# Taps, gates and modulation steps put in other places of a two-layer model with an RWKV block

## The chip, the cores and the metric

The kernel runs on one core of a Trainium2 chip. The metric is the device time of one execution in microseconds, taken as the median of several runs.

## The reference, cut to what matters

The input is one sequence of 256 positions with 1024 channels in float32. Two layers, each a mixer and a convolutional feed-forward block, are followed by a second block with adaptive modulation, an RWKV recurrence and a depthwise convolution.

```python
for i in range(2):                       # first block
    h = rmsnorm(x, norm_mix[i])
    x = x + (gla_mixer(h, ...) if i == 0 else attn_mixer(h, ...))
    x = x + conv_ffn(rmsnorm(x, norm_ffn[i]), ...)
def conv_ffn(h, w_up, w_conv, b_conv, w_down):
    u = conv3(h @ w_up) + b_conv         # depthwise, width 3
    val, gate = split(u)
    return (silu(gate) * val) @ w_down   # 2816 wide
# second block
mod = silu(c) @ ada_w + ada_b            # 1024 -> 3 x 1024
shift, scale, gate = split(mod)
h = rmsnorm(x, norm_g) * (1 + scale) + shift
c_val, c_gate, c_og, ts, r_og, g_conv, g_rwkv = split(h @ w_in)
u = causal_depthwise_conv(c_val * sigmoid(c_gate), conv_k) + conv_b  # 31 taps
y_conv = (silu(layernorm(u)) * silu(c_og)) @ w_conv_out
o = rwkv7_scan(token_shift(ts), ...)     # per head: state update, read-out
o = layernorm_per_head(o) + bonus
y_rwkv = (o * silu(r_og)) @ w_rwkv_out
m = sigmoid(g_conv) * y_conv + sigmoid(g_rwkv) * y_rwkv
x = x + gate * (m @ w_out)
out = rmsnorm(x, final_g)
```

## The kernel before, in words

Activations are kept with channels on the 128 partitions and the 256 positions along the free axis, in 8 chunks of 128 channels. Every large product is made in float32 accuracy from two reduced-precision parts, hi and lo, of both factors. `mm3` (L113 to L115) gives three products of 256 columns per chunk, `mm2` (L120, L123) one of 512 and one of 256 columns.

**Weights.** `Weights.load` (L77 to L80) brings each weight block into one of a ring of raw buffers by a DMA on SP's queue, strictly in program order (`issue_after`). ACT copies it to `hi` (L78), and DVE subtracts to get `lo` (L80). The DMA for a raw buffer waits until `lo` of the block that had the buffer last has been made.

**Order.** The kernel is written in one order. A scheduler arranges the instructions of each engine ahead of time. On the chip each engine runs its own list strictly in that order, so an instruction that waits holds up all that stand behind it.

**Stages.** The GLA mixer comes first: its rank products `gr` (L356) are the first that need weights, after warm-up products `warm` (L1331). Then `ffn0`, the attention layer and `ffn1`. A feed-forward block makes 22 pairs of `up` tiles with the width-3 convolution on ACT (L257) and DVE (L258, L259), a gated product `sg` (L263) and its split into `gg` (ACT L130, DVE L131), and then 8 `dn` tiles of 22 chunks each. `root_next` (L154) loads ACT's table of the square root ahead of the next norm.

**Modulation.** `ada` computes `silu(c) @ ada_w` in 24 steps of 1024 columns by 128 rows: a DMA of 512 KB into the same ring (`adaw`, L609) and one DVE instruction (L611 for the first of eight, L613 for the others). The table `AD` says after which loops of the stages a step is taken.

**The second block.** `inv` (from L845) inverts the triangular matrices of the recurrence on DVE, then makes the off-diagonal blocks by the cross products `zp` (L882) and `xp` (L892), with ACT copies between (L885, L874, L895). `chain` runs four chunks one after the other: `u`, the state `S` (`sp`, L924, then DVE L650), the output `op`, and after each second chunk the group norm `norm`, whose last step makes `yhi` (ACT L985) and `ylo` (DVE L990) for the products with `rwkv_out`. `fill` puts independent projections (`pj`) between these steps. The convolution has 8 channel chunks of 31 taps, each one DVE instruction (L1079, L1081). Chunks 5 to 7 (`CJ`) are bound behind the inverse. `cln` is its layer norm (`cmean` L1086, `nps_cv`, `rps_cv`) with the SiLU (L1095) and the gate `scog`, split into `yc`. `rout`, `cout` and `wout` are the last three projections. The gates are parked in DRAM and read back when wanted (`gri`, `gci`, `scogi`: DMA on SP, then a sigmoid or SiLU on ACT, L1010). `final` is the last norm with four output DMAs.

## Time and profile before

| what | value |
|---|---|
| median of 3 runs (lowest to highest) | 1013.92 us (1012.06 to 1015.05) |
| the profiled execution's own time | 1013.54 us |
| its span in the trace | 1011.7 us |
| mean granted TensorE clock | 0.983 of full |
| TensorE (PE) busy | 974.7 us, 96% |
| VectorE (DVE) busy | 832.3 us, 82% |
| ScalarE (ACT) busy | 611.0 us, 60% |
| bytes moved | 175.01 MB, mean 173 GB/s |

PE is busy for all but some 37 us of the span. A busy PE is not always at full speed: the granted clock is 0.5 or thereabouts in some short stretches, and there the same products take longer. So both the idle time and these stretches are to be read, and both are small against the span.

### The profile page before, as it was taken

Reading aid. Unit: us, or ns where it says so; the run is one execution under the profiler, and the core shown is the slowest. Engines: PE = TensorE matmul, PEld = TensorE weight load, DVE = VectorE, ACT = ScalarE, POOL = GpSimd, SP = SyncE. Lnnn points to the kernel's source line nnn. Section 1 sums busy time; section 2 is a strip of 40 time slices with the busy share of each in tenths; the row PEclk is TensorE's granted clock in tenths of the full one; section 3 lists DMA queues with packets and bytes.
Section 4 is the critical chain, followed back from the end, with each engine's and each line's share of the span. In section 5 each row is a group of like instructions: output and inputs, shape, how many; then the busy total and the mean of one; then the engine's idle time right before and its main releaser. Section 6 shows DMA issues by size and latency. Waiting matters only on the chain.

```text
span 1011.7 us, 19352 instructions
## 1 busy us (share of the span) xinstructions
PE 974.7 (96%) x7636; PEld 905.8 (90%) x7636; DVE 832.3 (82%) x1529; ACT 611.0 (60%) x1052; POOL 5.1 (0%) x15
## 2 busy tenths in 40 slices
PE   8999999999999999999999999999999999999796
PEld 7988899999888877999999889999988998898795
DVE  5956589888867886998888667999899898889795
ACT  6635666666544567676666456545676646745663
POOL 0000000000000000000000000000000000000000
PEclk8999999999999999999999999999999998999898
DMA  7738155556776861546656675455432362436451
GB/s 267 256 122 277 50 182 187 188 178 190 223 219 217 276 215 42 180 157 218 180 183 174 188 249 199 149 187 180 157 106 84 93 222 92 154 115 199 162 161 42
DMA packets 54442, 175.01 MB, mean 173 GB/s; under 512 B 6320, under 2 KB 12976, under 8 KB 53968
## 3 DMA queue, kind: packets, MB, share of 16 engines
q1 hardware_dynamic: 50464, 169.51, 52.7%
q10 hardware_dynamic: 3888, 4.27, 1.2%
q8 instruction: 60, 0.98, 0.4%
q14 instruction: 30, 0.25, 0.1%
HBM read 168.51 MB, written 5.24 MB: 172 GB/s over the span
## 4 chain that ended last, share of the span: by engine, by line
PE 79%; DVE 10%; DMA 4%; ACT 4%; issue 2%; ACTq 0%; DVEq 0%; SPq 0%
PE pj L113 8%; PE pj L115 8%; PE pj L114 8%; PE dn L120 8%; PE up L114 7%; PE up L115 7%; PE up L113 7%; PE pj L120 4%; PE dn L123 4%; DVE lo L80 3%; PE pj L123 2%; DMA adaw<-ada_w 2%; PE pt L113 2%; PE pt L114 2%; PE pt L115 2%
## 5 line engine op out<-in xcount | busy, mean ns | idle before, releaser
L78 ACT CAST hi<-raw 128x1024 fp32r<-128x1024 f32 (+2 forms) x286 | 295.0, 1034 | 243.2 <-PE pj L114 82.6
L80 DVE TENSOR_TENSOR lo<-raw,hi 128x1024 fp32r<-128x1024 f32 (+2 forms) x286 | 344.0, 1205 | 78.3 <-ACT hi L78 70.7
L114 PE MATMUL up<-h_f,hi 128*128 128x256 f32 x640 | 181.4, 284 | 0.5 <-DVE h_f L131 0.5
L113 PE MATMUL up<-h_f,hi 128*128 128x256 f32 x640 | 180.8, 283 | 0.3 <-ACT h_f L130 0.3
L115 PE MATMUL up<-h_f,lo 128*128 128x256 f32 x640 | 180.8, 283 | 0.0
L115 PE MATMUL pj<-h_s,lo 128*128 128x256 f32 x544 | 156.1, 287 | 1.7 <-DVE lo L80 1.7
L113 PE MATMUL pj<-h_s,hi 128*128 128x256 f32 x544 | 157.4, 290 | 0.0
L114 PE MATMUL pj<-h_s,hi 128*128 128x256 f32 x544 | 156.2, 287 | 0.0
L120 PE MATMUL dn<-gg,hi 128*128 128x512 f32 x352 | 124.9, 402 | 0.0
L114 PEld LDWEIGHTS up<-h_f,hi 128*128 128x128 f32 x640 | 122.8, 192 | 1.1 <-DVE h_f L131 1.1
L113 PEld LDWEIGHTS up<-h_f,hi 128*128 128x128 f32 x640 | 122.6, 192 | 0.5 <-ACT h_f L130 0.5
L115 PEld LDWEIGHTS up<-h_f,lo 128*128 128x128 f32 x640 | 122.8, 192 | 0.0
L115 PEld LDWEIGHTS pj<-h_s,lo 128*128 128x128 f32 x544 | 104.8, 193 | 2.6 <-DVE lo L80 1.9
L113 PEld LDWEIGHTS pj<-h_s,hi 128*128 128x128 f32 x544 | 104.9, 193 | 1.5
L114 PEld LDWEIGHTS pj<-h_s,hi 128*128 128x128 f32 x544 | 104.9, 193 | 1.1 <-issue 0.3
L1081 DVE SCALAR_TENSOR_TENSOR y<-u,long,y 128x233 f32<-128x233 f32 (+27 forms) x240 | 99.7, 469 | 0.7
L123 PE MATMUL dn<-gg,lo 128*128 128x256 f32 x352 | 97.1, 283 | 2.5 <-ACT gg L130 2.5
L120 PEld LDWEIGHTS dn<-gg,hi 128*128 128x128 f32 x352 | 66.2, 190 | 15.1
L123 PEld LDWEIGHTS dn<-gg,lo 128*128 128x128 f32 x352 | 67.0, 191 | 4.3 <-ACT gg L130 3.1
L257 ACT ACTIVATE y<-up,const 128x256 f32<-128x256 f32 x80 | 44.2, 556 | 1.9 <-DVE y L259 1.8
L259 DVE SCALAR_TENSOR_TENSOR y<-up,const,y 128x255 f32<-128x255 f32 x80 | 38.1, 479 | 1.2
L258 DVE SCALAR_TENSOR_TENSOR y<-up,const,y 128x255 f32<-128x255 f32 x80 | 37.9, 477 | 0.7 <-ACT y L257 0.7
(464 smaller groups left out, 1831.3 us busy)
## 6 DMA issues: line engine op xcount, KB each, us to landing
raw<-w_up SPq DMA_DIRECT2D x88, 512.0 KB, 4.1
raw<-w_down SPq DMA_DIRECT2D x32, 448.0 KB, 3.5
adaw<-ada_w SPq DMA_DIRECT2D x24, 512.0 KB, 4.5
raw<-w_down SPq DMA_DIRECT2D x16, 512.0 KB, 4.0
raw<-w_cvg SPq DMA_DIRECT2D x16, 512.0 KB, 4.1
raw<-gla_v SPq DMA_DIRECT2D x8, 512.0 KB, 5.1
raw<-gla_g SPq DMA_DIRECT2D x8, 512.0 KB, 3.7
raw<-gla_out SPq DMA_DIRECT2D x8, 512.0 KB, 4.8
```

The source lines that it names most:

```text
L78: nc.scalar.copy(hi[:, :w], raw[:, :w])
L80: nc.vector.tensor_tensor(out=lo[:, :w], in0=raw[:, :w], in1=hi[:, :w].bitcast(F32), op=ALU.subtract)
L113: nc.tensor.matmul(ps, lh, rh, start=start, stop=False)
L114: nc.tensor.matmul(ps, lh, rl, start=False, stop=False)
L115: nc.tensor.matmul(ps, ll, rh, start=False, stop=stop)
L120: wide = lambda: nc.tensor.matmul(ps, lhs[0], both, start=first, stop=last)
L123: nc.tensor.matmul(ps[:, 0], lhs[1], both[:, 0], start=False, stop=False)
L257: nc.scalar.activation(yb, ps[:, b, :], AF.Identity, scale=cw[:, 1, c:c + 1], bias=cw[:, 3, c:c + 1])
L258: nc.vector.scalar_tensor_tensor(out=yb[:, 1:], in0=ps[:, b, :T - 1], scalar=cw[:, 0, c:c + 1], in1=yb[:, 1:], op0=ALU.mult, op1=ALU.add)
L259: nc.vector.scalar_tensor_tensor(out=yb[:, :T - 1], in0=ps[:, b, 1:], scalar=cw[:, 2, c:c + 1], in1=yb[:, :T - 1], op0=ALU.mult, op1=ALU.add)
L1081: nc.vector.scalar_tensor_tensor(out=y[:, i:], in0=u[:, :T - i], scalar=w[:, j, 30 - i:31 - i], in1=y[:, i:], op0=ALU.mult, op1=ALU.add)
```

## The change

Seven edits are made at once.

- `gr`: two small products that nobody reads are put after each of the first seven chunks, six after the last (`g.idle`). `rstd_cols` runs its products in another order.
- `AD`: `ffn0` takes six modulation steps rather than eight, `ffn1` two rather than none; attention still takes eight, but each is two further on in the count.
- Convolution taps: chunks 5 to 7 come first, handed out in portions of 12, 6, 6 and eight times 8 inside `inv` and `chain` (`taps`); chunks 0 to 4 follow. The products `cmean` of chunks that are done are then free to stand in the chain.
- `zp`: the loop over halves is outside the loop over banks, and each bank and half has its own copy at once.
- `wout`: the square root's table is loaded after the last gate, and the last tile is made by `mm3` with one accumulator rather than `mm2` with two.
- `final`: five output DMAs, the last of one chunk, rather than four, the last of two.
- A switch that was off (`CT`) goes away.

```diff
@@ -157,9 +157,9 @@
 def rstd_cols(g, acc, name, eps=EPS):
 
     ps = g.ps.tile([P, 512], F32, name=f"nps_{name}")
-    for t in range(2):
-        for a in acc:
-            g.nc.tensor.matmul(ps[:, 2 * t:2 * t + 2], a[:, t * P:(t + 1) * P], g.ones[:, :2], start=a is acc[0], stop=a is acc[-1])
+    for a in acc:
+        for t in range(2):
+            g.nc.tensor.matmul(ps[:, 2 * t:2 * t + 2], a[:, t * P:(t + 1) * P], g.ones[:, :2], start=a is acc[0] and t == 0, stop=a is acc[-1], skip_group_check=True)
     return rsqrt(g, ps[:, :4], 1.0 / D, eps, name)
 
 
@@ -356,6 +356,7 @@
     ps = g.ps.tile([P, 512], F32, name="gr")
     for k in range(KD):
         mm3(nc, ps[:64, :T], (wh[:, k, :], wl[:, k, :]), (h[0][:, k, :], h[1][:, k, :]), k == 0, k == KD - 1)
+        g.idle(2 if k < KD - 1 else 6)
     for d in range(2):
         rows = slice(32 * d, 32 * d + 16)
         nc.vector.tensor_tensor(out=rT[rows, :], in0=ps[rows, :T], in1=rstd[rows, :], op=ALU.mult)
@@ -588,7 +589,7 @@
     out_project(g, I["attn_out"], o2)
 
 
-AD = dict(zip(("g", "f0", "a", "f1"), "11111111,11111111,11111111,00000000".split(",")))
+AD = dict(zip(("g", "f0", "a", "f1"), "11111111,00111111,11111111,00110000".split(",")))
 
 
 def step(g, where, i):
@@ -637,7 +638,6 @@
 CV = 16
 CJ = 5
 LAG = 2
-CT = 0
 PRE = dict(zip(("g", "f0", "a", "f1"), "00000000,00000000,00000000,00000000".split(",")))
 TB = 2
 ORDER = "low cvg pr pk pv prep inv gains chain cog gr gc conv cln rout cout wout"
@@ -874,15 +874,14 @@
             nc.scalar.copy(TTm[p0:p0 + 32, :, 32 * dg:32 * dg + 32], TD[p0:p0 + 32])
         zt = X2[:, 0]
         fill(1)
-        for b in range(2):
-            zp = psum.tile([P, 16, 32], F32, name=f"zp{b}")
-            for i in range(16):
-                for hf in range(2):
-                    o = 64 * hf + 32
-                    nc.tensor.matmul(zp[o:o + 32, i, :], Lb[64:96, hf, b, i, 32:], X2[64:96, hf, 16 * b + i, :], start=True, stop=True)
-            for hf in range(2):
-                o = 64 * hf + 32
-                nc.scalar.copy(zt[o:o + 32, 16 * b:16 * b + 16, :], zp[o:o + 32])
+        taps(12)
+        zp = [psum.tile([P, 16, 32], F32, name=f"zp{b}") for b in range(2)]
+        for hf in range(2):
+            o = 64 * hf + 32
+            for b in range(2):
+                for i in range(16):
+                    nc.tensor.matmul(zp[b][o:o + 32, i, :], Lb[64:96, hf, b, i, 32:], X2[64:96, hf, 16 * b + i, :], start=True, stop=True)
+                nc.scalar.copy(zt[o:o + 32, 16 * b:16 * b + 16, :], zp[b][o:o + 32])
             fill(1)
         for b in range(2):
             xp = psum.tile([P, 16, 32], F32, name=f"xp{b}")
@@ -894,6 +893,7 @@
                 o = 64 * hf
                 nc.scalar.copy(TTm[o:o + 32, 16 * b:16 * b + 16, 32:], xp[o:o + 32])
             fill(1)
+            taps(6)
 
 
     def chain():
@@ -917,6 +917,7 @@
                 for i in range(2):
                     nc.scalar.copy(VU[64:128, c, 8 * b + i:8 * b + 8:2, :], up[64 * i:64 * i + 64, i::2, :])
             fill(FC[2 * c])
+            taps(8)
             if c < 3:
                 sp = psum.tile([P, KD, 64], F32, name=f"sp{c}")
                 for hd in range(16):
@@ -940,6 +941,7 @@
             v.done = nc.scalar.copy(v.OT[:, :, cs], op)
             S = Sn
             fill(FC[2 * c + 1])
+            taps(8)
             if c % 2:
                 norm(c2)
 
@@ -1007,7 +1009,7 @@
         def get(j):
             t = sb.tile([P, T], F32, tag=name + "i", name=f"{name}i{j}")
             g.w.after(t, d[:, j, :])
-            nc.scalar.activation(t, t, f)
+            v.gate = nc.scalar.activation(t, t, f)
             return t
 
         setattr(v, name, get)
@@ -1060,25 +1062,38 @@
         for _ in range(CV):
             next(gates["cvg"])
 
-    def conv():
-        with ExitStack() as es:
-            conv_taps(es)
-
-    def conv_taps(es):
+    def chunks(js, es=None):
+
+        w = cst["conv_k"]
+        for j in js:
+            y, u = v.y[j], v.u[j]
+            behind = lambda: g.tc.issue_after(v.inv.ins) if j >= CJ else ExitStack()
+            with behind():
+                nc.vector.tensor_scalar(out=y, in0=u, scalar1=w[:, j, 30:31], scalar2=cst["conv_b"][:, j:j + 1], op0=ALU.mult, op1=ALU.add)
+            yield
+            for i in range(1, 31):
+                with behind():
+                    nc.vector.scalar_tensor_tensor(out=y[:, i:], in0=u[:, :T - i], scalar=w[:, j, 30 - i:31 - i], in1=y[:, i:], op0=ALU.mult, op1=ALU.add)
+                yield
+
+    def late():
         rest("cvg")
         v.ya = full("y")
         v.y = [v.ya[:, j, :] for j in range(KD)]
-        w = cst["conv_k"]
-        for j in range(KD):
-            y, u = v.y[j], v.u[j]
-            if j == CJ:
-                es.enter_context(g.tc.issue_after(v.inv.ins))
-            if CT:
-                nc.scalar.activation(y, u, AF.Identity, scale=w[:, j, 30:31], bias=cst["conv_b"][:, j:j + 1])
-            else:
-                nc.vector.tensor_scalar(out=y, in0=u, scalar1=w[:, j, 30:31], scalar2=cst["conv_b"][:, j:j + 1], op0=ALU.mult, op1=ALU.add)
-            for i in range(1, 31):
-                nc.vector.scalar_tensor_tensor(out=y[:, i:], in0=u[:, :T - i], scalar=w[:, j, 30 - i:31 - i], in1=y[:, i:], op0=ALU.mult, op1=ALU.add)
+        yield from chunks(range(CJ, KD))
+
+    late = late()
+
+    def taps(n):
+
+        for _ in range(n):
+            next(late, None)
+
+    def conv():
+        for _ in late:
+            pass
+        for _ in chunks(range(CJ)):
+            pass
 
     def cln():
         mps = bank("cmean")
@@ -1123,14 +1138,16 @@
         gated(I["conv_out"], v.yc, v.gc)
 
     def wout():
+        root_next(g, v.gate)
         g.x = full("x2")
         g.w.after(g.x, g.xs)
 
-        def ev(j, ps):
-            for b in range(2):
+        def ev(j, ps, n=2):
+            for b in range(n):
                 nc.vector.scalar_tensor_tensor(out=g.x[:, j, :], in0=ps[:, b], scalar=g.mod[:, 16 + j:17 + j], in1=g.x[:, j, :], op0=ALU.mult, op1=ALU.add)
 
-        project_both(g, I["w_out"], v.mh, ev)
+        project_both(g, I["w_out"][:KD - 1], v.mh, ev)
+        project(g, I["w_out"][KD - 1:], (v.mh[:, 0], v.mh[:, 1]), lambda j, ps: ev(KD - 1, ps.unsqueeze(1), 1))
 
     steps = dict(low=low, pk=pk, pr=pr, pv=pv, prep=prep, inv=inv, chain=chain, gains=gains, cvg=cvg, conv=conv, cln=cln,
                  rout=rout, cout=cout, wout=wout)
@@ -1147,7 +1164,7 @@
     r = rstd_cols(g, sumsq(g, "final"), "final")
     scale(KD - 1)
     rstd = spread(g, r, "final")
-    for a, n in ((0, 1), (1, 2), (3, 3), (6, 2)):
+    for a, n in ((0, 1), (1, 2), (3, 2), (5, 2), (7, 1)):
         o = g.sb.tile([P, n, T], F32, name=f"out{a}")
         nc.vector.tensor_tensor(out=o, in0=xg[:, a:a + n, :], in1=rstd.unsqueeze(1).to_broadcast([P, n, T]), op=ALU.mult)
         nc.sync.dma_start(g.O["outT"][:, a:a + n, :], o)
@@ -1327,8 +1344,12 @@
         nc.scalar.preload_act_table(AF.Silu)
         nc.vector.memset(g.ones, 1.0)
         warm = g.ps.tile([P, P], F32, name="warm")
-        for _ in range(WARM):
-            nc.tensor.matmul(warm, g.ones, g.ones, start=True, stop=True)
+        def idle(n):
+            for _ in range(n):
+                nc.tensor.matmul(warm, g.ones, g.ones, start=True, stop=True)
+
+        g.idle = idle
+        idle(WARM)
         nc.scalar.activation(g.silu_c, cst, AF.Silu)
         g.cst = {}
         g.cst["norm_mix0"], g.cst["ident"] = first[:, :KD], first[:, KD:]
```

DVE where `ffn1` passes from its last `up` tiles to its first `dn` tiles (`lo`: weight blocks; `gg`: the split of the gated product; `x<-dn`: the finished tile), before:

```order
L131 TENSOR_TENSOR gg_4506<-sg_20_6060,gg_4506 128x256
L259 SCALAR_TENSOR_TENSOR y_1_21_6126<-up_21_6065,const_3541,y_1_21_6126 128x255
L80 TENSOR_TENSOR lo_6230<-raw_6228,hi_6229 128x896
L258 SCALAR_TENSOR_TENSOR y_1_21_6130<-up_21_6065,const_3541,y_1_21_6130 128x255
L259 SCALAR_TENSOR_TENSOR y_1_21_6130<-up_21_6065,const_3541,y_1_21_6130 128x255
L80 TENSOR_TENSOR lo_6250<-raw_6248,hi_6249 128x896
L263 TENSOR_TENSOR sg_21_6134<-sg_21_6134,y_1_21_6126 128x256
L131 TENSOR_TENSOR gg_4506<-sg_21_6134,gg_4506 128x256
L276 TENSOR_TENSOR x<-dn_0_6140,x 128x256 x2
```

and now:

```order
L80 TENSOR_TENSOR lo_6234<-raw_6232,hi_6233 128x896
L131 TENSOR_TENSOR gg_4510<-sg_20_6064,gg_4510 128x256
L258 SCALAR_TENSOR_TENSOR y_1_21_6134<-up_21_6069,const_3545,y_1_21_6134 128x255
L259 SCALAR_TENSOR_TENSOR y_1_21_6134<-up_21_6069,const_3545,y_1_21_6134 128x255
L80 TENSOR_TENSOR lo_6254<-raw_6252,hi_6253 128x896
L263 TENSOR_TENSOR sg_21_6138<-sg_21_6138,y_1_21_6130 128x256
L614 SCALAR_TENSOR_TENSOR ada_3924<-adaw_7_6343,long,ada_3924 128x1024
L131 TENSOR_TENSOR gg_4510<-sg_21_6138,gg_4510 128x256
L276 TENSOR_TENSOR x<-dn_0_6144,x 128x256 x2
```

The last `ada` step of `ffn1` stands between `sg_21` and `gg_21`. In `ffn0` the order was `ada` (step 3), `sg_21`, `gg_21`, and is now `sg_21`, `gg_21`, `ada` (step 1).

DVE ahead of the products with `rwkv_out` (`OT`: the recurrence's output, `y<-u`: a tap), before:

```order
L1081 SCALAR_TENSOR_TENSOR y<-u,long,y 128x240
L1081 SCALAR_TENSOR_TENSOR y<-u,long,y 128x239
L650 TENSOR_TENSOR OT<-OT,gnb_10316 128x4x128
L1081 SCALAR_TENSOR_TENSOR y<-u,long,y 128x238
L650 TENSOR_TENSOR OT<-OT,srog 128x4x128
L650 TENSOR_TENSOR OT<-OT,gnb_10329 128x4x128
L984 TENSOR_TENSOR OT<-OT,vf 128x4x128
L650 TENSOR_TENSOR OT<-OT,srog 128x4x128
L1081 SCALAR_TENSOR_TENSOR y<-u,long,y 128x237
L984 TENSOR_TENSOR OT<-OT,vf 128x4x128
L990 TENSOR_TENSOR ylo<-OT,yhi 128x1024 x2
```

and now:

```order
L1076 SCALAR_TENSOR_TENSOR y<-u,long,y 128x229
L80 TENSOR_TENSOR lo_10912<-raw_10910,hi_10911 128x1024
L650 TENSOR_TENSOR OT<-OT,gnb_10425 128x4x128
L1076 SCALAR_TENSOR_TENSOR y<-u,long,y 128x228
L650 TENSOR_TENSOR OT<-OT,srog 128x4x128
L650 TENSOR_TENSOR OT<-OT,gnb_10438 128x4x128
L986 TENSOR_TENSOR OT<-OT,vf 128x4x128
L650 TENSOR_TENSOR OT<-OT,srog 128x4x128
L1076 SCALAR_TENSOR_TENSOR y<-u,long,y 128x227
L986 TENSOR_TENSOR OT<-OT,vf 128x4x128
L992 TENSOR_TENSOR ylo<-OT,yhi 128x1024
L1076 SCALAR_TENSOR_TENSOR y<-u,long,y 128x226
L992 TENSOR_TENSOR ylo<-OT,yhi 128x1024
```

The subtraction for a weight block stands ahead of the first `OT<-OT,gnb`, a tap stands between the two `ylo`, and on ACT a table load and a gate stand between the two `yhi`.

ACT from the SiLU of the convolution branch on (L1010, now L1012: a gate; L1095, now L1110: the SiLU), before:

```order
L143 ACTIVATE r_cv<-m_cv 128x4
L78 CAST hi_11182<-raw_11181 128x1024
L1095 ACT_TABLE_LOAD
L1095 ACTIVATE y<-y,long 128x256 x3
L130 CAST yc_10718<-y 128x256 x2
L1095 ACTIVATE y<-y,long 128x256 x2
L130 CAST yc_10718<-y 128x256
L1095 ACTIVATE y<-y,long 128x256 x2
L1010 ACTIVATE scogi_10746<-scogi_10746 128x256
L1010 ACTIVATE scogi_10754<-scogi_10754 128x256
L1095 ACTIVATE y<-y,long 128x256
L130 CAST yc_10718<-y 128x256 x2
```

and now, the end of the same stretch:

```order
L1110 ACTIVATE y<-y,long 128x256
L130 CAST yc_10738<-y 128x256 x2
L1012 ACTIVATE scogi_10782<-scogi_10782 128x256
L1110 ACTIVATE y<-y,long 128x256
L1012 ACT_TABLE_LOAD
L1012 ACTIVATE gri_11081<-gri_11081 128x256
L130 CAST yc_10738<-y 128x256
L1012 ACT_TABLE_LOAD
L1012 ACTIVATE scogi_10790<-scogi_10790 128x256
L1012 ACTIVATE scogi_10798<-scogi_10798 128x256
L78 CAST hi_11088<-raw_11087 128x1024
L130 CAST yc_10738<-y 128x256 x2
```

Before, one table load (`ACT_TABLE_LOAD`) stands between `r_cv` and the last `yc`; now there are four (two stand in the rows left out), and the cast of `hi_11088`, the first weight block of `conv_out`, stands behind all four. Before, the cast of that block stood ahead of `r_cv`.

## Rows read from the trace of the kernel before

**Rows 1.** The page, part 1: busy us (share of the span) and instructions.
```profile
PE 974.7 (96%) x7636; PEld 905.8 (90%) x7636; DVE 832.3 (82%) x1529; ACT 611.0 (60%) x1052; POOL 5.1 (0%) x15
```

**Rows 2.** By stretch: PE, PEld, DVE, ACT, POOL busy (instructions), granted clock, DMA.
```profile
820.00:830.00 10.00, 10.00 (x86) 10.00 (x85) 9.73 (x17) 5.90 (x8) 0.00 (x0) 1.00 0.94 307
15.60:20.70 5.10, 5.10 (x25) 5.10 (x26) 2.69 (x5) 2.36 (x3) 0.00 (x0) 0.50 0.94 343
280.00:283.50 3.50, 3.50 (x13) 2.94 (x13) 2.89 (x4) 1.22 (x2) 0.00 (x0) 0.52 0.43 129
949.10:956.00 6.90, 5.06 (x21) 4.71 (x21) 3.62 (x11) 4.34 (x11) 0.00 (x0) 0.51 0.76 273
```

**Rows 3.** What PE waited for, whole span: total us, times, longest.
```profile
PE pj L113 <- ACT yc L130: 4.5, 2, 3.5
...
PE dn L123 <- ACT gg L130: 2.5, 1, 2.5
...
PE kTp L531 <- DVE akr L483: 1.5, 1, 1.5
...
PE pj L114 <- DVE ylo L990: 1.3, 1, 1.3
...
PE rps_cv L170 <- DVE r_cv L147: 1.2, 1, 1.2
```

**Rows 4.** Timeline of PE at the start: start, us, line, out<-in, count [idle before].
```profile
4.62 1.92 PE L1331 MATMUL warm<-long 128*128 128x128 f32 x8
...
11.70 0.38 PE L113 MATMUL pj<-ph_g,hi 128*128 128x256 f32 x1 [1.27 <-ACT hi L78]
...
13.04 0.39 PE L115 MATMUL pj<-ph_g,lo 128*128 128x256 f32 x1 [0.84 <-DVE lo L80]
```

**Rows 5.** Timeline of DVE ahead of the down products of ffn0.
```profile
277.27 1.28 DVE L613 SCALAR_TENSOR_TENSOR ada<-adaw,long,ada 128x1024 f32<-128x1024 f32 x1 [2.71 <-DMA adaw<-ada_w]
```

**Rows 6.** Timeline of SP there.
```profile
272.29 0.33 SPq L609 DMA_DIRECT2D adaw<-ada_w  x1
```

**Rows 7.** Timeline of DVE ahead of the down products of ffn1.
```profile
551.84 1.09 DVE L80 TENSOR_TENSOR lo<-raw,hi 128x896 fp32r<-128x896 f32 x1
...
556.19 0.42 DVE L131 TENSOR_TENSOR gg<-sg,gg 128x256 fp32r<-128x256 f32 x1 [0.61 <-ACT gg L130]
```

**Rows 8.** Timeline of ACT around the cross products zp.
```profile
844.81 4.22 ACT L874 COPY TT<-LT 32x1024 f32<-32x1024 f32 x4
```

**Rows 9.** Timeline of DVE after the inverse, to the first chain state.
```profile
848.90 8.73 DVE L1081 SCALAR_TENSOR_TENSOR y<-u,long,y 128x255 f32<-128x255 f32 x22
861.10 0.69 DVE L650 TENSOR_TENSOR S<-sp,long 128x512 f32<-128x512 f32 x1 [3.46 <-PE sp L924]
```

**Rows 10.** Timeline of PE ahead of the first rwkv_out tile.
```profile
915.59 3.18 PE L1086 MATMUL cmean<-y,long 128*128 128x256 f32 x14
```

**Rows 11.** Timeline of DVE there.
```profile
911.91 1.22 DVE L80 TENSOR_TENSOR lo<-raw,hi 128x1024 fp32r<-128x1024 f32 x1
...
919.48 2.36 DVE L990 TENSOR_TENSOR ylo<-OT,yhi 128x1024 fp32r<-128x1024 f32 x2
```

**Rows 12.** Timeline of ACT between the convolution norm and the first conv_out tile.
```profile
946.05 1.28 ACT L1095 ACT_TABLE_LOAD   x1
947.66 1.58 ACT L1095 ACTIVATE y<-y,long 128x256 f32<-128x256 f32 x3 [0.34 <-DVE y L650]
949.99 0.74 ACT L130 CAST yc<-y 128x256 fp32r<-128x256 f32 x2 [0.74 <-DVE y L650]
...
954.88 0.72 ACT L1010 ACTIVATE scogi<-scogi 128x256 f32<-128x256 f32 x2 [1.82 <-DMA scogi<-scogd]
```

**Rows 13.** Timeline of ACT at the final norm.
```profile
1001.85 1.28 ACT L143 ACT_TABLE_LOAD   x1
```

**Rows 14.** Timeline of DVE there.
```profile
999.98 1.00 DVE L1131 SCALAR_TENSOR_TENSOR x<-pj,long,x 128x256 f32<-128x256 f32 x2 [0.51 <-PE pj L120]
...
1005.53 2.48 DVE L1152 TENSOR_TENSOR out<-xg,rps_final 128x256 f32<-128x256 f32 x4 [1.38 <-PE rps_final L170]
```

## The prediction

> **What bounds the kernel now.** I read the page first: PE is busy for 974.7 of 1011.7 us, 96% [rows 1], so nearly all of the time is products that the change leaves alone (it adds 20 small ones). What can move is PE's idle time and the stretches at the lower clock. The stretches came second. At full clock 86 products took 10.00 us, 0.116 each; at granted clock 0.50, 25 took 5.10 us, 0.204 each [rows 2]. So a busy microsecond at the lower level (1.2 rather than 2.4 GHz) loses 1 - 0.116/0.204 = 0.43 us. Third came PE's waits, which name the seams: the SiLU branch (`yc`, 4.5 in two waits), `gg` (2.5), `akr` (1.5), `ylo` (1.3), `r_cv` (1.2) [rows 3]. The low-clock stretches behind `gg` and behind `r_cv` and `yc` are in [rows 2], and single waits of 1.3 to 1.5 have none there. Last I read the lists of DVE, ACT and SP at these seams. Because PE's work stays, each term below is idle time or low clock that goes or comes. A plus is a gain.
>
> **The start.** 20 idle products are added. Eight took 1.92 us [rows 4], so 0.24 each and 4.8 us, or some 0.22 and 4.4 where they follow closely. PE waited 1.27 and 0.84 for the first big weight block [rows 4]; these 2.1 us are covered now. If the products hold the clock, 5.10 x 0.43 = 2.2 us of the first stretch come back [rows 2], and about 0.7 of the 1.7 us ahead of it, which I estimate to be at the lower level too. That gives 2.1 + 2.2 + 0.7 - 4.4 = **+0.5**. If the clock falls all the same it is 2.1 - 4.8 = -2.7, and at best +1. The other order in `rstd_cols` has the same eight products: nothing.
>
> **ffn0.** DVE waited 2.71 us for step 3, whose weights SP had issued at 272.29 and which landed at 277.27, 4.98 later [rows 5, 6]. `sg` and `gg` stood behind it, and PE waited 2.5 [rows 3], followed by 3.5 us at clock 0.52 [rows 2], 3.5 x 0.43 = 1.5 lost. Now the step stands behind `gg`, and what it holds up is the evacuation of the tile and the next `lo`, due only when the next tile of 22 chunks is done. **+4.0**, between 2 and 4.5.
>
> **ffn1.** The same pattern is put here, where it wasn't. The second step stands ahead of the last `gg`, and its DMA is issued once the `lo` that began at 551.84 has freed a raw buffer [rows 7], so at about 552.9. With 4.98 us on the way [rows 6] and 1.28 for the step [rows 5] it ends at 559.2, and `gg` at 559.6. Before, `gg` began at 556.19 and ended at 556.6 [rows 7], and PE did not wait. That is 3.0 us late, or 2.1 if the landing is a microsecond quicker. The nearest row is the wait in ffn0, 2.5 [rows 3]; I take that, and its low clock of 1.5: **-4.0**, between 0 and -4.6. What is queued behind the step on DVE is `gg`, two evacuations and the next `lo`; PE waits for `gg`.
>
> **Attention.** Two steps rather than four precede `akr`, so the 1.5 us of `kTp` [rows 3] should go. Four steps of 1.28 [rows 5] now lie in the first half of the softmax, where one lay. DVE is in PE's way there, and the output weights come later. I take **+0.5**, between -4 (three more steps, 3.8) and +1.5.
>
> **The inverse.** Before, ACT's four copies of TT, 4.22 us from 844.81 [rows 8], stood between the first and the other three copies of `zp`, so the first state waited: DVE stood idle for 3.46 us until 861.10, though its taps (22 in 8.73 us from 848.90) were done at 857.6 [rows 9]. By halves, the copies of `zp` no longer stand behind TT. The state can't come before the taps, which DVE has in front of it either way, so at most 3.5 is to be had. The first half of `zp` still waits for its transpose on DVE. **+3.0**, between 1 (the clock drops there as before) and 3.5.
>
> **The chain.** Taps are now handed out ahead of each later state, about 17 ahead of the second at 8.73/22 = 0.40 [rows 9], 6.8 us on DVE, where before other DVE work of some 2 us stood. What covers this on PE is products `cmean` of finished chunks, 4 to 6 pairs, which before stood at the chain's end (14 in 3.18 us, 0.45 a pair [rows 10]), and projections. I take **-0.5**; it is -2 if the cover runs out, +1 if it doesn't.
>
> **Ahead of rwkv_out.** Here that cover is gone. Before, 14 `cmean` instructions, 3.18 us, lay between the group norm and `yhi` [rows 10], and PE then waited 1.3 for `ylo` [rows 3]. Now one or two pairs are left there, so 2.2 more are idle. A `lo` of 1.22 [rows 11] stands ahead of the first `OT`, and a tap of 0.40 [rows 9] between the two `ylo` (2.36 for both [rows 11]). Idle: 2.2 + 1.2 + 0.4 = **-3.8**; 0 if PE finds other products. Such a pair of waits was followed by a low stretch of 6.9 us at `yc` [rows 2]; 6.9 x 0.43 = 3.0 at most, 0 at least. As four products lie between the two waits I take half, **-1.5**.
>
> **conv_out.** Before: waits of 1.2 and 4.5 [rows 3] and 5.06 busy us at clock 0.51 [rows 2], 2.2 lost, 7.9 in all. Now the norm's products come earlier, and the gates' DMAs with them, so neither `r_cv` nor the gate that ACT waited 1.82 for [rows 12] holds PE up. But ACT has four table loads of 1.28 [rows 13], 8 SiLU of 1.58/3 = 0.53 [rows 12], 6 casts of 0.37 [rows 12], eight gates of the 0.36 that two of them show (0.72) [rows 12] and two weight casts of about 1.1, like the `lo` in [rows 11], ahead of the last two `yc`: 5.1 + 4.2 + 2.2 + 2.9 + 2.2 = 16.6 us from `r_cv` on. The cast of the first `conv_out` block is the last of these. Less 2.4 from there to `rps_cv` and 0.8 of overlap, it is ready 13.4 us behind `rps_cv`, while PE has 74 products x 0.12 = 9.1 us until it wants it. Idle 4.3, then 0.9 for its `lo`, and 2.2 at the lower clock: 7.4 against 7.9, **+0.5**; +2.7 with the clock up, -2 with ACT's waits.
>
> Against this order speaks the Trainium skill, ScalarE: Activation LUTs, What ACT_TABLE_LOAD costs: a switch to another set of functions costs 1283 ns and about 1380 ns of drain, some 2.66 us in all. Before, the load at 946.05 ended at 947.33 and the next SiLU began at 947.66, of which 0.34 was a wait for DVE [rows 12], so this trace doesn't show the drain. By that page, as an estimate, the seam would take 4 x 1.38 = 5.5 us more, and the sum 1018.5; it ends where the rival of the table switches does, and I count it in that chance with 0.02.
>
> **The tail.** The square root's table, 1.28 us from 1001.85 [rows 13], is loaded earlier, and one of two evacuations (1.00 for both [rows 14]) goes, 0.45. PE's last tile does the same multiplications as 24 products of 0.116 [rows 2] rather than eight wide and eight narrow ones, which I count as equal. The outputs move the same bytes in one more DMA, with a smaller last one; I price that at 0, half a microsecond either way. **+1.7**, between 0.5 and 2.2.
>
> **The sum.** 0.5 + 4.0 - 4.0 + 0.5 + 3.0 - 0.5 - 3.8 - 1.5 + 0.5 + 1.7 = +0.4, some 1013.1 from the profiled execution's 1013.5. That execution lies 0.4 below the median of the runs shown; I say 1013.0.
>
> **The rivals.**
>
> *The new waits fall short* (faster). The step in ffn1 lands in time, and the low clock behind the entry to rwkv_out and at conv_out doesn't come. For it: DMAs of 512 KB differ in their time on the way, and single waits of 1.3 to 1.5 had no low stretch behind them. Against it: DVE's list in ffn1 is the one that stalled in ffn0. 1013.0 - 4.0 - 1.5 - 2.2 = 1005.3.
>
> *ACT's table switches hold conv_out up* (slower). ACT's list from `r_cv` to the first `conv_out` block takes longer than its parts, because a gate or a product of DVE comes late between two switches, as the gate did that ACT waited 1.82 for [rows 12]. With two or three such waits, 5 us, 1018. It decides once the cast ends more than 17.4 us behind `rps_cv`, for then 4 us are lost beyond my term. Against it: the gates' DMAs are issued earlier.
>
> *Attention's softmax behind modulation steps* (slower): -3.8 rather than +0.5, 1017.3. For it: DVE keeps its list. Against it: the steps' weights are there early, and PE has other products.
>
> *The idle products don't hold the clock*: -2.7 rather than +0.5, 1016.2, inside the forecast's own case.
>
> **How the numbers follow.** Forecast 1013.0 with its own range of 1010 to 1016.5: 0.40. The new waits fall short: 0.37. Table switches: 0.15. Softmax: 0.08. A measurement of this kernel can tell about 0.3%, 3 us, from no change; by the cases faster has 0.37, within 0.3% 0.40, slower 0.23. The range goes from 1004 (the first rival, a little beyond its sum) to 1018 (the switches' price).
>
> **What would show it.** In the trace after: no wait of PE for `gg` in ffn0, one of 2 to 3 us in ffn1; the first state by 859 on the clock of before; the wait ahead of `rwkv_out` 4 to 5 us in two pieces; PE waiting for the first weight block of `conv_out`, not for `yc`; no table load behind the last square. Wrong would be a long wait in a stage that I price at nothing, or full clock where I have put the lower one.

## The result and the profile after

The changed kernel takes 1025.58 us (median of 4 runs, 1021.93 to 1029.62) against 1014.48 us for the kernel before in the same comparison. The ratio is 1.0114 [1.0094, 1.0133]: slower by 1.1%, some 11 us, and outside the range of the prediction. The profiled execution took 1025.45 us, its span is 1023.4 us, and the mean granted clock is 0.977, where it was 0.983.

Part 1 of the page of after, against [rows 1]:

```profile
PE 983.7 (96%) x7684; PEld 913.6 (89%) x7684; DVE 832.5 (81%) x1529; ACT 614.8 (60%) x1055; POOL 4.8 (0%) x15
```

PE is busy for 9.0 us more and idle for 2.7 us more (39.7 against 37.0). Of the 48 records more, 40 are the 20 idle products and 8 the narrower products of the last tile. Two idle products (four records, a product leaves two) take 0.37 us from start to start, so the 20 are some 3.7 us. Of the other 5.3 us, some 3.0 are the lower clock: PE was busy for 33.8 us at 0.50, where it was for 26.8 before, and a busy microsecond there loses 0.43. Most of the rest are the `zp` products, which take longer in their new order (see below). What PE waited for, over the whole span of after (columns: total us, times, longest), against [rows 3]:

```profile
PE zp L883 <- DVE X L869: 5.1, 1, 5.1
PE pj L113 <- ACT hi L78: 4.5, 1, 4.5
PE pj L113 <- ACT yhi L987: 3.4, 1, 3.4
...
PE nps_a L162 <- ACT sq_a L185: 1.1, 1, 1.1
...
PE pj L114 <- DVE ylo L992: 0.8, 1, 0.8
...
PE dn L120 <- DVE gg L131: 0.7, 1, 0.7
```

The first row had no counterpart in the forecast; before, the same wait was much shorter:

```profile
PE zp L882 <- DVE X L869: 1.8, 2, 1.2
```

The second and third are waits that were forecast. `gg` in `ffn0` and `akr` are gone. Stretches of PE in after (columns as in [rows 2]):

```profile
15.60:20.70 5.10, 5.10 (x46) 5.10 (x45) 3.24 (x7) 3.19 (x6) 0.00 (x0) 1.00 0.99 372
843.00:856.60 13.60, 12.35 (x151) 11.51 (x151) 13.54 (x26) 5.40 (x8) 0.00 (x0) 0.50 0.11 40
928.30:938.60 10.30, 6.81 (x28) 6.34 (x29) 9.23 (x19) 3.90 (x7) 0.00 (x0) 0.50 0.64 200
962.50:969.30 6.80, 4.22 (x18) 3.93 (x19) 4.93 (x7) 6.76 (x11) 0.00 (x0) 0.50 0.11 24
```

The start now runs at full clock: 46 products where [rows 2] has 25. The price comes late: three long stretches at 0.50 follow the waits for `zp`, for `yhi` and for the first `conv_out` block. The third has its like in [rows 2], and the first had this one before, half as long:

```profile
843.30:850.20 6.90, 6.90 (x118) 6.55 (x111) 6.90 (x15) 5.89 (x7) 0.00 (x0) 0.51 0.12 21
```

The second figure of a row is PE's busy time in the stretch; the rest is idle.

I cut both traces at the first product of each stage and compared lengths in us. A plus is a gain, each figure is rounded by itself, and the sum is the difference of the spans.

| stage on PE | before | after | gain |
|---|---|---|---|
| start to first `dn` of ffn0 | 266.2 | 265.0 | +1.2 |
| ffn0's `dn`, to `nps_a` | 68.2 | 64.1 | +4.1 |
| attention and ffn1's `up` | 213.4 | 214.4 | -0.9 |
| ffn1's `dn` | 62.2 | 64.9 | -2.7 |
| preparation of the recurrence, to the last `nl` | 188.0 | 189.6 | -1.6 |
| last `nl` to first `zp` | 42.5 | 46.3 | -3.8 |
| `zp` to the chain's first `u` | 14.1 | 15.6 | -1.5 |
| chain, to first product of `yhi` | 64.0 | 71.0 | -7.0 |
| `yhi` to first product of `yc` | 31.8 | 33.7 | -1.9 |
| `yc` to `mh` to `nps_final` | 49.3 | 48.7 | +0.6 |
| `nps_final` to the end | 11.9 | 10.1 | +1.8 |

Up to the recurrence the kernel after is even with the one before: the last `nl` stands at 798.0 us in both. All of the loss lies between there and `yc`, 14.2 us, and three parts of the change meet in that stretch. One execution each of two kernels below (`b_tail` 1186.9 us, `b_zp` 1032.4) ran slow at a lower clock and is left out of the ratios.

### The profile page after: what moved, and what is told of

Read it like the earlier page. It is cut to its first block, busy times and chain, and to the rows that moved or that the text cites. A ratio compares the mean times of both kernels' runs of the same rounds, so it can differ in the third digit from the quotient of the medians.

```text
span 1023.4 us, 19458 instructions
## 1 busy us (share of the span) xinstructions
PE 983.7 (96%) x7684; PEld 913.6 (89%) x7684; DVE 832.5 (81%) x1529; ACT 614.8 (60%) x1055; POOL 4.8 (0%) x15
## 4 chain that ended last, share of the span: by engine, by line
PE 54%; DVE 7%; ACT 4%; DMA 2%; issue 1%; DVEq 0%; ACTq 0%
PE pj L115 7%; PE pj L113 7%; PE pj L114 7%; PE up L114 4%; PE up L115 4%; PE up L113 4%; PE dn L120 3%; PE pj L120 2%; DVE lo L80 2%; PE dn L123 2%; PE pj L123 1%; ACT hi L78 1%; DMA scogd<-scogo 1%; PE pt L113 1%; PE pt L115 1%
## 5 line engine op out<-in xcount | busy, mean ns | idle before, releaser
L80 DVE TENSOR_TENSOR lo<-raw,hi 128x1024 fp32r<-128x1024 f32 (+2 forms) x286 | 343.7, 1205 | 83.6 <-ACT hi L78 78.2
L115 PE MATMUL pj<-h_s,lo 128*128 128x256 f32 x544 | 158.4, 292 | 1.7 <-DVE lo L80 1.7
L113 PEld LDWEIGHTS pj<-h_s,hi 128*128 128x128 f32 x544 | 106.5, 196 | 1.4
L114 PEld LDWEIGHTS pj<-h_s,hi 128*128 128x128 f32 x544 | 106.5, 196 | 0.8 <-issue 0.3
L1076 DVE SCALAR_TENSOR_TENSOR y<-u,long,y 128x253 f32<-128x253 f32 (+23 forms) x240 | 101.0, 463 | 0.9
L614 DVE SCALAR_TENSOR_TENSOR ada<-adaw,long,ada 128x1024 f32<-128x1024 f32 x21 | 26.9, 1281 | 16.9 <-DMA adaw<-ada_w 16.9
L259 DVE SCALAR_TENSOR_TENSOR y<-up,const,y 128x255 f32<-128x255 f32 x80 | 38.1, 479 | 1.2
```

The costliest lines, as they stand in the source:

```text
L80: nc.vector.tensor_tensor(out=lo[:, :w], in0=raw[:, :w], in1=hi[:, :w].bitcast(F32), op=ALU.subtract)
L113: nc.tensor.matmul(ps, lh, rh, start=start, stop=False)
L114: nc.tensor.matmul(ps, lh, rl, start=False, stop=False)
L115: nc.tensor.matmul(ps, ll, rh, start=False, stop=stop)
L259: nc.vector.scalar_tensor_tensor(out=yb[:, :T - 1], in0=ps[:, b, 1:], scalar=cw[:, 2, c:c + 1], in1=yb[:, :T - 1], op0=ALU.mult, op1=ALU.add)
L614: nc.vector.scalar_tensor_tensor(out=acc, in0=r, scalar=sc[:, k:k + 1], in1=acc, op0=ALU.mult, op1=ALU.add)
```

## The experiments

A kernel named `a_...` is the kernel after with one part undone; `b_...` is the kernel before with one part done; `best1...` is explained below. Ratios are to the kernel before on the same chip, with 95% intervals.

### The parking buffers behind the inverse

The wait for `zp` led me to ACT's list ahead of it. There the gates are parked: ACT copies `pj` to `scogo` or `gro` (one of two buffers with the tag `spill`) and issues the DMA to DRAM. ACT's rows, first before, then after:

```profile
821.67 0.37 ACT L1004 COPY scogo<-pj 128x256 f32<-128x256 f32 x1
822.06 0.33 ACTq L1005 DMA_DIRECT2D scogd<-scogo  x1
...
824.31 0.37 ACT L1004 COPY scogo<-pj 128x256 f32<-128x256 f32 x1
...
831.19 0.37 ACT L1004 COPY gro<-pj 128x256 f32<-128x256 f32 x1 [1.15 <-DMA scogd<-scogo]
```

```profile
821.62 0.37 ACT L1006 COPY scogo<-pj 128x256 f32<-128x256 f32 x1
822.02 0.33 ACTq L1007 DMA_DIRECT2D scogd<-scogo  x1
...
826.62 0.37 ACT L1006 COPY scogo<-pj 128x256 f32<-128x256 f32 x1 [2.27 <-DMA scogd<-scogo]
...
831.76 0.37 ACT L1006 COPY scogo<-pj 128x256 f32<-128x256 f32 x1 [3.24 <-DMA scogd<-scogo]
```

Before, the copy at 824.31 runs 2.25 us after a DMA is issued and waits for nothing, and the one at 831.19 waits for the landing of the DMA two back, issued at 824.70: copies take the two buffers in turn. After, the copy at 826.62 waits for the DMA issued just ahead of it, at 822.02, so both use one buffer. Behind such a copy on ACT stand weight casts `hi`; DVE's `lo` waits for those, in the middle of the inverse. DVE after (the profile of before shows no wait of DVE from 800 to 846 us):

```profile
828.55 1.22 DVE L80 TENSOR_TENSOR lo<-raw,hi 128x1024 fp32r<-128x1024 f32 x1 [1.31 <-ACT hi L78]
...
834.05 1.23 DVE L80 TENSOR_TENSOR lo<-raw,hi 128x1024 fp32r<-128x1024 f32 x1 [2.34 <-ACT hi L78]
```

1.31 + 2.34 = 3.65 us, and the first `zp` is 3.8 us late. No line of the diff touches the copies or their buffers. To test it, `a_spill` gives the two buffers out by name:

```diff
-            t = sb.tile([P, T], F32, tag="spill", bufs=2, name=f"{name}o{j}")
+            t = sb.tile([P, T], F32, tag=f"spill{j % 2}", bufs=1, name=f"{name}o{j}")
```

> The changed kernel, with the two parking buffers of the gates taken in turn by name, so that each copy waits for the DMA two back and not for the last one. Theory (in the changed kernel ACT's copies into the parking buffer waited 2.3 and 3.2 us for the DMA just issued, and held weight casts, and so the inverse on DVE, up): these waits go, the wait of TensorE ahead of the cross products falls from 5.1 to about 1.3 us, and the time by 3.8, to about 1021.8. Rival 1 (the long wait also brought the long stretch at the lower clock behind it, 13.6 us): 3.8 and some 3 to 4 more, about 1018. Rival 2 (the DMAs themselves were slow, whichever buffer they wait for): 1025.

Measured: 1018.02 us, 1.0052 [1.0024, 1.0080]. ACT's copies wait for no DMA any more, and PE's wait for `zp` is:

```profile
PE zp L883 <- DVE X L869: 1.4, 1, 1.4
```

The waits went, as the theory said, but the time fell by more than its 3.8 us, to where rival 1 put it: that one line gives back half of the whole loss (1.0114 to 1.0052). In its profile 3.8 us of it lie from `nl` to `zp`, 0.8 from there to the first `u`, where the stretch at 0.50 is 10.2 us long rather than 13.6, and 1.6 in the preparation, where after had a low stretch from 767.9 to 771.3 that this run didn't have (see the last section). The next kernel, `b_idle`, tells where the pattern comes from: it is before, with the idle products and the new order in `rstd_cols`, nothing else.

```diff
+        g.idle(2 if k < KD - 1 else 6)
...
-    for t in range(2):
-        for a in acc:
+    for a in acc:
+        for t in range(2):
```

> The kernel before with the 20 idle products among the rank products and the other order in the norm's column sums, alone. Theory (the idle products shift the planner's times, and by that alone the parking buffers are given out so that each copy waits for the DMA just issued): the start gains 1.2, the inverse ends 3.7 later, and the time is 1016 to 1018. Rival (the idle products act at the start only): 1012.8, with the inverse on time.

Measured: 1017.20 us, 1.0035 [1.0011, 1.0059]: slower, though its start is 1.3 us shorter. ACT's parking copies, and PE's wait:

```profile
824.67 0.37 ACT L1005 COPY scogo<-pj 128x256 f32<-128x256 f32 x1 [2.12 <-DMA scogd<-scogo]
...
831.17 0.37 ACT L1005 COPY scogo<-pj 128x256 f32<-128x256 f32 x1 [4.61 <-DMA scogd<-scogo]
```

```profile
PE zp L883 <- DVE X L870: 6.2, 1, 6.2
```

So these two edits make the copies at 825 us wait, though the idle products stand between 8 and 16 us on the clock and neither edit touches these buffers. The pattern is in every kernel here that has the two edits and shares the buffers by rotation (after, `b_idle`, `a_nozp`, `a_notaps`), and in none of the others. What changes, by the waits, is which of the two buffers a copy is given when the lists are made. Why was not settled, and the idle products and the order in `rstd_cols`, which each later norm uses as well, weren't run apart.

### Cross products by halves

`a_nozp` is after with `zp` made bank by bank again; `b_zp` is before with `zp` by halves.

```diff
+        zp = [psum.tile([P, 16, 32], F32, name=f"zp{b}") for b in range(2)]
+        for hf in range(2):
+            o = 64 * hf + 32
+            for b in range(2):
...
+                nc.scalar.copy(zt[o:o + 32, 16 * b:16 * b + 16, :], zp[b][o:o + 32])
```

> The changed kernel with the cross products again bank by bank, taps as in the changed kernel. Theory (by halves, ACT makes its four copies of TT after the last copy of zp rather than between, so that xp waits for them): the first u comes 1.5 us earlier behind the inverse, and the time is about 1024. Rival 1 (the halves are what brings the long stretch at the lower clock): 1020. Rival 2 (the halves help, as the prediction had it): 1028.

> The kernel before with the cross products by halves, alone. Theory (removing the halves from the changed kernel shortened u to yhi by 4.5 us, so they cost as much here): 1017. Rival 1 (the prediction's term): 1010.5. Rival 2 (the halves lose only with the taps between): 1013.5.

Measured: `a_nozp` 1019.26 us, 1.0058 [1.0030, 1.0086], so 0.6 of the 1.1% goes when this edit is undone. `b_zp` 1020.83 us, 1.0059 [1.0034, 1.0084], so the edit alone costs 0.6%. ACT in `b_zp`, against [rows 8]:

```profile
845.08 0.58 ACT L883 COPY X<-zp 32x512 f32<-32x512 f32 x1 [2.77 <-PE zp L882]
846.09 0.58 ACT L883 COPY X<-zp 32x512 f32<-32x512 f32 x1 [0.44 <-PE zp L882]
849.24 0.58 ACT L883 COPY X<-zp 32x512 f32<-32x512 f32 x1 [2.56 <-PE zp L882]
851.59 0.58 ACT L883 COPY X<-zp 32x512 f32<-32x512 f32 x1 [1.77 <-PE zp L882]
852.19 4.23 ACT L874 COPY TT<-LT 32x1024 f32<-32x1024 f32 x4
857.90 2.37 ACT L893 COPY TT<-xp 32x512 f32<-32x512 f32 x4 [1.47 <-PE xp L890]
```

The copies of `zp` don't stand behind `TT` any more. Now the 4.23 us of `TT` stand behind all four copies and end at 856.42, and the main body of `xp`, which reads both, begins at 856.67 (852.52 before). That looks like the cost, but most of the difference is older: `b_zp` is 3.36 us late at its first `zp` already (843.88 against 840.52), since attention took 3.5 us longer in this profile. Counted from the first `zp`, the main body of `xp` moved from 12.0 to 12.8 us and `u` from 14.1 to 14.9, and the profile shows no wait of PE ahead of either, before or now: the projections fill the time. DVE's first state `S`, which has 3.46 us of idle time ahead of it in [rows 9], has in `b_zp` and in after:

```profile
865.93 0.69 DVE L650 TENSOR_TENSOR S<-sp,long 128x512 f32<-128x512 f32 x1 [6.22 <-PE sp L922]
```

```profile
867.43 0.69 DVE L650 TENSOR_TENSOR S<-sp,long 128x512 f32<-128x512 f32 x1 [6.68 <-PE sp L925]
```

Counted from the first `zp`, the state comes at 20.6 us before, 22.1 in `b_zp` and 23.2 in after. This is DVE's wait; PE's idle time between the first `zp` and the first `yc` is 7.2 us before and 7.6 in `b_zp`.

What costs PE is the `zp` products themselves. Bank by bank, they write two groups of 32 partitions in turn; by halves, 32 products in a row write the same group. PE in `b_idle` (bank by bank), then in after (by halves), both inside a stretch at 0.50:

```profile
846.21 3.62 PE L883 MATMUL zp<-X,VU 32*32 32x32 f32 x124
```

```profile
844.25 3.59 PE L883 MATMUL zp<-X,VU 32*32 32x32 f32 x64 [5.14 <-DVE X L869]
```

The same time holds half as many records. At full clock it is so too: `best1` (below, bank by bank) makes 124 in 2.21 us from 839.15, and `b_zp` 64 in 2.18 from 843.88, while its `xp`, which goes on writing two groups in turn, has 124 in 2.21 from 856.67. All 128 take 3.5 us before and 6.0 in `b_zp`, 2.5 in `best1` and 5.6 in `best1_zp`, 4.0 in `a_nozp` and 7.4 in after: 2.5, 3.1 and 3.4 more by halves. From the first `zp` to the first `yc` the kernel with the halves is 4.9, 4.1 and 3.7 us longer in these three pairs. What is left, 2.4, 1.0 and 0.3, is no more than the lower clock takes: by halves there are one or two more stretches of 3.4 us at 0.50 in each pair. That the halves bring those isn't shown: behind the same bank-by-bank code the stretch is 3.4 us long in `best1`, 6.8 in `best1_noad` and 10.2 in `b_tail`.

`a_nozp` came in near its rival 1 (1020), but its stretch behind `zp` is as long as in after, 13.6 us. Nor did its theory come: counted from the first `zp`, its `u` is 0.6 us later than after's (16.2 against 15.6), not 1.5 earlier.

### The taps in portions

`a_notaps` is after with the taps in one piece, `b_taps` is before with the portions.

```diff
+        taps(12)
...
+            taps(6)
...
+            taps(8)
...
+        yield from chunks(range(CJ, KD))
```

> The changed kernel with the convolution's taps again in one piece behind the chain's steps, cross products by halves as in the changed kernel. Theory (taps ahead of the states delay the second state by some 6 us and take the cover of the norm's products away from the entry to rwkv_out, where TensorE waited 3.4 and 0.8): that entry's wait falls to about 1.3 in all, and the time by 4 to 6, to 1020. Rival (DVE's list there is full either way and the taps only change places): within 1.5 us of the changed kernel, 1025.

> The kernel before with the late taps handed out in portions, alone (cross products bank by bank, no idle products). Theory (the taps take the cover of the norm's products away from the entry to rwkv_out, and bring the table switches ahead of the first conv_out block): TensorE waits 3.4 and 0.8 at the entry, 4.5 ahead of conv_out, and the stretches from u to yhi and from yhi to yc are together 3 to 5 us longer than before, so 1017. Rival (it is only together with the halves of the cross products that the taps lose): within 1.5 us of the kernel before.

Measured: `b_taps` 1019.54 us, 1.0049 [1.0016, 1.0082]: half a per cent by itself. `a_notaps` 1022.80 us, 1.0090 [1.0062, 1.0117]: undoing it in the kernel after gives back a quarter of a per cent, less than the other two, and the two intervals overlap. Its profile still has the wait for `zp` (4.9) and the low stretch behind it. `b_taps` shows the two seams of after to a tenth:

```profile
PE pj L113 <- ACT hi L78: 5.8, 2, 4.5
PE pj L113 <- ACT yhi L989: 3.4, 1, 3.4
```

PE in after at the entry to `rwkv_out`, against [rows 10]:

```profile
926.89 0.70 PE L1101 MATMUL cmean<-y,long 128*128 128x256 f32 x2
930.95 1.22 PE L113 MATMUL pj<-yhi,hi 128*128 128x256 f32 x4 [3.36 <-ACT yhi L987]
933.00 0.58 PE L114 MATMUL pj<-ylo,hi 128*128 128x256 f32 x1 [0.83 <-DVE ylo L992]
933.38 0.42 PE L115 MATMUL pj<-yhi,lo 128*128 128x256 f32 x1
```

Two `cmean` instructions are left of the 14 that covered this wait. The products behind it take 0.42 us, which take 0.28 at full clock.

### The tail

`b_tail` is before with the three edits at the end.

```diff
+        root_next(g, v.gate)
...
+        project_both(g, I["w_out"][:KD - 1], v.mh, ev)
+        project(g, I["w_out"][KD - 1:], (v.mh[:, 0], v.mh[:, 1]), lambda j, ps: ev(KD - 1, ps.unsqueeze(1), 1))
...
-    for a, n in ((0, 1), (1, 2), (3, 3), (6, 2)):
+    for a, n in ((0, 1), (1, 2), (3, 2), (5, 2), (7, 1)):
```

> The kernel before with the square root's table loaded after the last gate, the last tile with one accumulator and five output DMAs, alone. Theory (the tail of the changed kernel is 1.7 us shorter from the last norm's first product on, and 0.2 more behind it): 1011.5. Rival (the table load lands in a seam of conv_out on ACT, or the fifth DMA costs what the load gave): 1013.4.

Measured: 1014.34 us, 0.9999 [0.9969, 1.0029]: no change that can be told. PE's end is 1.6 us shorter, but the stretch from the first `w_out` product to `nps_final` is 1.7 longer. ACT's list there holds the early table load:

```profile
979.84 1.28 ACT L154 ACT_TABLE_LOAD   x1
981.14 1.05 ACT L78 CAST hi<-raw 128x1024 fp32r<-128x1024 f32 x1
```

It stands ahead of a weight cast and of the last `mh`, and PE waits for `mh` in two pieces (0.6 and 0.4) where before it didn't; in `best1`, which has the same edit, it is three (0.37, 0.62 and 0.41), 1.4 us. In after one of these waits is left, 0.24 us.

### Keeping what gains

`best1` is before with the idle products, the order in `rstd_cols`, `AD`, the tail and the parking buffers by name; the taps and `zp` stay as before. Three more runs put one part to it or take one away: `best1_taps` adds the taps in portions, `best1_zp` adds `zp` by halves, `best1_noad` takes `AD` back. Their edits are the ones above and the line of `AD`.

> The kernel before with the idle products, the modulation steps' new places and the tail, with the parking buffers taken in turn by name, without the taps' portions and without the halves. Theory (what loses is the buffers, the taps and the halves, and the other edits gain 1.2 at the start, about 0.4 by the modulation steps and 1.9 in the tail): 1009.5 to 1010.5. Rival (the low clock behind the cross products grows by itself, as it did in the runs without the buffer waits): 1013.

> The version best1 (idle products, modulation steps, tail, parking buffers by name) and the late taps in portions. Theory (the taps cost what they cost alone, 5 us: the entry to rwkv_out waits 3.4 and 0.8, conv_out 4.5, with longer low-clock stretches behind both): 1016. Rival (part of their loss alone came with the seams of the kernel before): 1013.

> The version best1 and the cross products by halves. Theory (the halves cost in each company: u comes no earlier than 0.6 us, fewer projections lie beside the way to it, and the time from the cross products to yhi is 3 to 4 us longer): 1014.5. Rival (their loss alone was a longer low-clock stretch that came by chance): 1011.

> The version best1 with the modulation steps where the kernel before has them. Theory (what the new places gain in ffn0, 4.0 from the start of the down products to attention, is given back by 0.9 in attention and 2.7 in ffn1): 1011.5, within 1.5 us of best1, with the wait for gg in ffn0 and for akr back. Rival (the prediction's term for ffn1 was too large, so that the places gain 3): 1014.

| kernel | us | ratio |
|---|---|---|
| `best1` | 1011.07 | 0.9973 [0.9953, 0.9992] |
| `best1_taps` | 1015.46 | 1.0021 [1.0000, 1.0042] |
| `best1_zp` | 1016.90 | 1.0023 [1.0000, 1.0045] |
| `best1_noad` | 1011.36 | 0.9983 [0.9962, 1.0004] |

On this base the taps cost 0.48% and the halves 0.50%, as they did alone (0.49% and 0.59%); as differences of two ratios these are good to some 0.3% either way. `AD` can't be told from nothing by the times. In the traces, `best1` reaches the norm behind `ffn1` at 606.5 us and `best1_noad` at 608.0, which would be 1.5 us, less than the runs scatter.

`best2` is `best1` with the table load moved from `wout` into `final`, behind the first scaled chunk:

```diff
     def wout():
-        root_next(g, v.gate)
...
-    for k in range(KD - 1):
+    root_next(g, scale(0))
+    for k in range(1, KD - 1):
         scale(k)
```

> The version best1 with the square root's table loaded behind the first scaled chunk of the final norm rather than behind the last gate, where it stood ahead of a weight cast. Theory (TensorE's waits of 0.6, 0.4 and 0.4 at the first w_out tiles go): 1009.7. Rival (the load takes its 1.28 us from the next weight cast there as well): 1011.

Measured: 1008.79 us, 0.9956 [0.9934, 0.9978]. It is faster than the kernel before, and than the one after by about 1.6%. ACT in `best2`:

```profile
978.11 1.05 ACT L78 CAST hi<-raw 128x1024 fp32r<-128x1024 f32 x1 [1.66 <-PE pj L120]
979.16 0.51 ACT L1146 ACTIVATE xg<-x,long 128x256 f32<-128x256 f32 x1
979.69 1.28 ACT L154 ACT_TABLE_LOAD   x1
```

The load lies where ACT had been idle for 1.66 us just before, and PE's waits for `mh` are gone. Its interval overlaps that of `best1`, so the times alone don't show the step from `best1` to `best2`.

## Why the prediction was wrong

Worked out from the ratios, the parts alone cost 3.5 us (idle products), 5.0 (taps), 6.0 (halves) and 0 (tail): 0.35%, 0.49%, 0.59% and nothing of 1014. `AD` gains 1 us by the difference of two ratios, which is less than their intervals. That is some 13.5 us, against 11 or 12 measured together; since each has an interval of 2.5 to 3 us either way, the parts add up. The steps, in the order of the prediction:

- **The start** (+0.5, though its terms add up to 0.6): right in sign. The clock held, and the stage gained 1.2. The price of the products was right by luck: [rows 4] shows records, two for each product, so eight of them are four products, at a pace that the idle products then beat (3.7 us for 20, where I had 4.4). The step that failed is that I looked for a cost only where the products run, and put the order in `rstd_cols` at "nothing". The two together moved waits on two buffers 800 us later, at 3.5 us net (`b_idle`). The copies stand in the same order on ACT before and after; only what they wait for differs.
- **ffn0** (+4.0): the wait for `gg` went, with its low clock. The stage gained 4.1, but 1.7 of it are 16 small `adaps` products that now stand in `ffn1`. Really +2.4, since new waits of 0.62 (`lo`) and 0.57 us (`nacc_a`) came.
- **ffn1** (-4.0): the mechanism came, much smaller. SP, DVE and PE in after:

```profile
548.72 0.33 SPq L610 DMA_DIRECT2D adaw<-ada_w  x1
```

```profile
553.16 1.28 DVE L614 SCALAR_TENSOR_TENSOR ada<-adaw,long,ada 128x1024 f32<-128x1024 f32 x1 [1.86 <-DMA adaw<-ada_w]
554.37 0.42 DVE L131 TENSOR_TENSOR gg<-sg,gg 128x256 fp32r<-128x256 f32 x1
```

```profile
554.84 0.73 PE L120 MATMUL dn<-gg,hi 128*128 128x512 f32 x2 [0.72 <-DVE gg L131]
```

The DMA is issued behind the `lo` of [rows 7], as forecast (this stage runs 4.3 us earlier on the clock of after), and landed 4.44 us later, where I had 4.98 from [rows 6]. `gg` ends at 554.79; on this clock it ended at 556.61 - 4.3 = 552.3 before, so it is 2.5 late (forecast 3.0). But PE waited 0.72 and the clock held. The step that failed is "the nearest row is the wait in ffn0": I took DVE's lateness for PE's wait. On PE four chunks of the second tile, 1.55 us from 552.57, now stand ahead of the product that waits. Of the stage's -2.7, 1.7 are the products from `ffn0`; really -1.0. The two terms were mis-sized by 1.6 and 3.0, with opposite signs.
- **Attention** (+0.5): measured -0.9. `akr`'s wait is gone, but the layer's norm waits 1.1 for a square at its start, where before it waited for nothing. `b_tail`, whose code there is that of before, has 0.8 of it, so this is in part scatter between runs.
- **The inverse** (+3.0): wrong in sign, -6 alone. The step that failed is "so the first state waited": I took 3.46 us of DVE's idle time for a gain of PE. From the first `zp` to `yhi` PE was busy for 77.0 of 78.2 us before, so 3 us of idle time were not there to be had. And I put the products in their new order at no price; they take 2.5 to 3.4 us more. My lower bound of +1 excluded a loss, and no row did. The state didn't come earlier either: forecast by 859, it came at 867.4. That is 6.3 behind the 861.1 of before: 3.7 because the first `zp` was late, 2.6 behind that.
- **The chain, the entry and conv_out** (-0.5, -3.8, -1.5, +0.5, in all -5.3): right in the sum, in part by luck. Alone the taps cost 5.0. The entry waited 3.36 + 0.83 = 4.19 in two pieces (forecast 4 to 5), which is 2.9 more than the 1.33 of before; I had 3.8. The low clock behind it was mis-sized: 6.81 busy us x 0.43 = 2.9, the upper bound, not half of it. The two errors cancel.
- **conv_out and the rival of the switches.** PE waited for the first weight block, as forecast, and not for `yc`: 4.55 + 0.47 (forecast 4.3 + 0.9; 74 x 0.12 is 8.9, not the 9.1 of my sum, which makes it 4.5). The cast ended 14.0 us behind `rps_cv`; I had 13.4, and the rival decides at 17.4. So the time of 1018 and more did not come from there. ACT's loads in after:

```profile
949.10 1.28 ACT L1012 ACT_TABLE_LOAD   x1
950.39 0.72 ACT L1012 ACTIVATE gri<-gri 128x256 f32<-128x256 f32 x2
951.13 1.28 ACT L1110 ACT_TABLE_LOAD   x1
952.42 1.59 ACT L1110 ACTIVATE y<-y,long 128x256 f32<-128x256 f32 x3
```

A load takes 1.28 us. The second starts 0.02 us behind the gates ahead of it (950.39 + 0.72 = 951.11), and a function starts 0.01 us behind each load. The Trainium skill (ScalarE: Activation LUTs, What ACT_TABLE_LOAD costs) gives 1283 ns, which agrees, and a drain of about 1380 ns beside it, which these switches don't show on either side.
- **The tail** (+1.7): `nps_final` to the end gained 1.8, as worked out. The term left out what the load is put ahead of: a weight cast at a seam where PE has no slack. From `mh` to `nps_final` this took back 0.5 in after and 1.7 in `b_tail`.

Of the sum, then, the taps and the tables came as forecast. Two terms, one that I had not seen and one with the wrong sign, make the miss: +0.5 to -3.5 for the idle products and +3.0 to -6 for the halves, 13 us, where 12.6 lie between forecast and result. The tail's 1.7, taken back in part by its own load, and `AD`, a little better than forecast, are smaller. None of the rivals named either. The slow side of the range rested on ACT's switches, a mechanism that I had already priced in the forecast, when the open question was the stage that the change writes in another order, and a wait that no row of the kernel before could show.

## What to carry to other kernels

An engine's idle time ahead of an instruction is a gain only where the engine that bounds the kernel waits too: here DVE waited 3.46 us for the state while PE had other products. When products are put in another order, ask what the order itself costs: `zp` took about twice as long per product at the same clock. When instructions are added or reordered, compare what each later buffer waits for, not only the order of the instructions; a pool that rotates two buffers can hand them out otherwise, and buffers given out by name don't depend on it. Moving cover (here `cmean`) earlier uncovers the wait that it covered, and the lower clock behind that wait cost as much as what the wait had grown by (2.9 us each).
